# Two hybrid mixer and MLP layers: a smaller scratch for dynamic transfers, deeper buffers, and a new order at the turn, in the tails and in the last chunk

## The chip, the cores and the metric

The kernel runs on one core of a Trainium2 chip. The metric is the device time of one launch in microseconds. A core has five engines, each with a queue of its own that it works through in order: PE (TensorE, matrix products), DVE (VectorE), ACT (ScalarE), POOL (GpSimd) and SP (SyncE, which here issues every transfer).

## The reference

768 tokens of width 1024 (256 of a context, 512 latent) go through two layers. In the last layer only the latent tokens are put out.

```python
for i in range(DEPTH):
    mix_l, mix_c = mixer(modulate(x_l, sh1_l, sc1_l), modulate(x_c, sh1_c, sc1_c), ...)
    x_l = layer_norm(ALPHA * x_l + g1_l * mix_l)
    x_l = layer_norm(ALPHA * x_l + g2_l * sq_relu_mlp(modulate(x_l, sh2_l, sc2_l), w1[i], w2[i]))
    # the context tokens likewise, but not in the last layer
```

The mixer projects its input once and splits it. One part is a conformer convolution: a gate, a depthwise convolution of 31 taps, a layer norm and swish. The other is a state-space scan (SSD) in both directions, over chunks of 128 tokens, in four groups of four heads: per chunk an intra-chunk product with a decay matrix, and a product of the chunk's C with the state of the chunks before it, in either direction. The scan's output is gated, normed per group, joined with the convolution's and projected back. The MLP squares a ReLU between two products of 1024 x 4096.

## The kernel before, in words

All products keep float32 accuracy: each operand is split into a high and a low part, and a product is three matmul passes. A weight goes through four steps as a *unit* of 128x1024: SP loads it into a tile `raw` (two of them), ACT casts the high part into `spl` or `splx` (L346), DVE or POOL subtracts it for the low part (L347), PE uses both.

The program is written as one sequence, and a scheduler with priorities lays it out per engine; a tile pool's `bufs` says how many copies of a tile may be alive, so it sets how early a producer may run. Small steps are put into a list (`later`) and taken off it at each `tick` between blocks of matmuls. The order on each engine is fixed when the program is built.

The stages, by their time in the profile: the modulation and first products (to 48 us), mixer of layer 0 (48 to 422), its *tail* (422 to 486), in which the last group's scan runs beside the first products of the output projection (`pa<-spl,cr`, L935), output projection (to 583), MLP of layer 0 (to 1107), the *turn* (1107 to 1177: the norm of the last MLP chunk, the split input `Hc` and `Hl` of layer 1, and the first products of its mixer), mixer of layer 1 (to 1441), its tail (to 1486), output projection (to 1562), MLP (to 1890) and the end.

The tiles that matter here. `xb` is a chunk's x and B with tokens on partitions, `fb` the feature-wise B or C of a group. `b` (tag b0) and `E` are the two directions' decay matrices of a chunk; SP loads their rows (L747), ACT takes the exponentials (L750, L754). `xd` holds x times the decay for the states (L728, on POOL), and under the same tag `to` holds a chunk's product with the states times its decay (L783, on DVE). `y` is a chunk's output:

```python
y  = x * cbd                  # POOL, L787
y += to[:, d] for each d        # L790: POOL, in the last group (g == 3) DVE
y += pd                         # DVE, L791; pd is the intra-chunk product in PSUM
y *= gz                         # DVE, L792; then its squares on ACT (L795)
```

Then POOL takes a group norm's `rsy`, ACT scales y (L804), PE transposes it (L811), ACT stores it (L711).

In the MLP, hidden units go through in eight chunks. In the last layer's chunk 7 the gate row `gr` is multiplied into the four w2 units (L340, on POOL, called the fold), so that the output needs no multiplication by the gate; the folded tile is `raw`. The row norm after an output projection or an MLP takes statistics on DVE (`bst`, `bve`), the reciprocal root `rsy` on POOL (L366), scales the rows on ACT (L876) and transposes them on PE (L886) into `Hc` or `Hl` by `to_feature`.

Of the kernel before, what the change touches and what calls it, by code (L numbers as in the profile page):

```python
# [7 lines left out]
F32 = mybir.dt.float32  # L8
# [14 lines left out]
DEPTH = 2  # L23
# [4 lines left out]
NPV = 288  # L28
HALVED = 228

GZB, XBB, YB, EB, TB, FXB, FBB, XDB, B0B, RAWB = 4, 6, 4, 3, 2, 2, 3, 2, 2, 2
BGR = 4
SQV = (1, 2, 3)
TAILV = 1
BGP = 100
GSUB = 1
DSUB = "SS"
# [6 lines left out]
FILLM = 4  # L44
MODP = 50
MODLAG = 6
SIDE = 5
FILL = (2, 4)
LOOK = (2, 2)
# [31 lines left out]
def block(ctx, tc, a):  # L81
# [28 lines left out]
    def pb():  # L110
        bank["b"] += 1
        if bank.get("mix"):
            if bank["b"] % 4 == 0:
                return bank["A"].tile([128, 512], F32, tag="A", name="pb")
            return (bank["B"] if bank["b"] % 4 == 2 else psB).tile([128, 512], F32, tag="B", name="pb")
        return (bank["B"] if "B" in bank and bank["b"] % 3 == 0 else psB).tile([128, 512], F32, tag="B", name="pb")
# [121 lines left out]
    def later(lag, fn, group=None):  # L238
        side.append((clock["t"] + lag, fn, group))
# [84 lines left out]

    ostate = {"late": True, "n": 0}

    def emit_unit():
        i = state["next"]
        u = plan[i]
        if u[0] == "out" and state["hid"] is not None and i % 2:  # L330
            raw = state["hid"].tile([128, 1024], F32, tag="raw", name="raw", bufs=2)
        else:
            raw = rawp.tile([128, 1024], F32, tag="raw", name="raw")
        dst = raw
        if u[0] in ("w2", "out"):
            dst = raw.rearrange("p (k c) -> p k c", k=2)
        Q.dma_start(dst, unit_src(u))
        if u[0] == "w2" and u[1] == DEPTH - 1 and u[2] == 7 and FOLD:
            g = state["gate"][:, None, u[3] * 512:(u[3] + 1) * 512].to_broadcast([128, 2, 512])
            (G if FOLD == 1 else V).tensor_tensor(dst, dst, g, op=MUL)  # L340
        state["n"] += 1
        if state["x"] is not None and state["n"] % 4 == 0:
            s = state["x"].tile([128, 2, 1024], F32R, tag="splx", name="splx")
        else:
            s = splp.tile([128, 2, 1024], F32R, tag="spl", name="spl")
# [53 lines left out]
    def mixer(l, full, Hc, Hl, m1, m2, head=None):  # L399
# [313 lines left out]
        def ssd(g, P):  # L713
# [54 lines left out]
            def output(c):  # L768
                Hs = X["H"]
                x = P["XB"][c][:, 0:256]  # L770
                W = X["W"][c]
                pd = pb()
                for h in range(4):
                    T.matmul(pd[:, h * 64:(h + 1) * 64], lhsT=W[:, h], rhs=x[:, h * 64:(h + 1) * 64],
                             start=True, stop=True)
                dirs = [(d, k) for d, k in ((0, c), (1, rev(c))) if k > 0]
                po = pb()
                for d, k in dirs:
                    T.matmul(po[:, d * 256:(d + 1) * 256], lhsT=P["C"][:, c * 128:(c + 1) * 128],
                             rhs=Hs[:, k - 1, d * 256:(d + 1) * 256], start=True, stop=True)  # L780
                d0, d1 = dirs[0][0], dirs[-1][0] + 1
                to = m2.tile([128, 2, 256], F32, tag="xd", name="to", bufs=XDB)
                V.tensor_tensor(to[:, d0:d1].rearrange("p d (h e) -> p d h e", h=4),  # L783
                                po[:, d0 * 256:d1 * 256].rearrange("p (d h e) -> p d h e", h=4, e=64),
                                D["ecs"][:, d0:d1, c, hs:hs + 4, None].to_broadcast([128, d1 - d0, 4, 64]), op=MUL)
                y = m2.tile([128, 256], F32, tag="y", name="y", bufs=YB)
                G.tensor_tensor(y.rearrange(h4, h=4), x.rearrange(h4, h=4),  # L787
                                X["cbd"][c][:, 0:4, None].to_broadcast([128, 4, 64]), op=MUL)
                for d, _ in dirs:
                    E2.tensor_tensor(y, y, to[:, d], op=ADD)  # L790
                V.tensor_tensor(y, y, pd[:, 0:256], op=ADD)  # L791
                V.tensor_tensor(y, y, P["gz"][c // 2][:, (c % 2) * 256:(c % 2 + 1) * 256], op=MUL)  # L792
                if c % 2 == 0:
                    X["ss"][c // 2] = m2.tile([128, 2], F32, tag="ssq", name="ssq", bufs=3)
                S.activation(to[:, 0], y, AF.Square, scale=1.0 / 16, accum_out=X["ss"][c // 2][:, c % 2:c % 2 + 1])  # L795
                X["y"][c] = y
# [78 lines left out]
        for j in range(2):  # L875
            S.activation(rts[j], rts[j], AF.Identity, bias=nb[:, j:j + 1], scale=y[:, j:j + 1])  # L876

    def to_feature(rts, Hd, t0, AB, group):
        n = 256

        def piece(k2):
            tp = pb()
            for i in range(2):
                kt = 2 * k2 + i
                for j, rt in enumerate(rts):
                    T.transpose(tp[:, i * 256 + j * 128:i * 256 + (j + 1) * 128], rt[:, kt * 128:(kt + 1) * 128], ident)  # L886
            for i in range(2):
                tmp = small.tile([128, 512], F32, tag="misc", name="tmp")
                split_h(Hd, 2 * k2 + i, t0, n, tp[:, i * 256:i * 256 + n], AB[0], AB[1], tmp[:, :n],
                        nB=AB[2])  # L890

        for k2 in range(4):
            later(0, lambda k2=k2: piece(k2), group)


    def outproj(l, cats, is_ctx, t0, pairs, xsrc, xdst, op, o2, group):
# [90 lines left out]
    def mlp(l, Hc, Hl, begin, residual, finish, fp):  # L987
# [33 lines left out]
        for ch in range(8):  # L1021
            hid = []
            if ch == RBEG:
                begin()
            if ch == 0:
                ws = []
                for m in range(4):
                    w = weight(("w1", l, m), 0)
                    ws.append(w)
                    hd = new_hid()  # L1030
                    hid.append(hd)
                    ps = pa()
                    parts = []
                    if Hc is not None:
                        cols(ps[:, 0:256], w, Hc, 0, 256)
                        parts.append((ps[:, 0:256], 0, 256))
                        tick(False)
                    cols(ps[:, 256:512], w, Hl, 0, 256)
                    parts.append((ps[:, 256:512], n0, n0 + 256))
                    act(hd, parts, 0, n0 + 256, m)  # L1040
                    tick(False)
                flush("h")
                for m in range(4):
                    ps = pa()
                    cols(ps[:, 0:256], ws[m], Hl, 256, 512)
                    act(hid[m], [(ps[:, 0:256], n0 + 256, n)], n0 + 256, n, m)
                    tick(False)
            else:
                for m in range(4):
                    w = weight(("w1", l, ch * 4 + m))  # L1050
                    hd = new_hid()
                    hid.append(hd)
                    parts = []
                    if Hc is not None:
                        ps = pa()
                        cols(ps[:, 0:256], w, Hc, 0, 256)
# [127 lines left out]
    for l in range(DEPTH):  # L1184
# [19 lines left out]
        with tc.tile_pool(name=f"x_{l}", bufs=1, reuse_waits="tile") as sx, \  # L1204
# [77 lines left out]
            def finish(t, ac, ps, hf, sl):  # L1282
# [26 lines left out]
                    nH["c"] = hp.tile([128, 8, 2, NCX], F32R, tag="Hc", name="Hc")  # L1309
                elif "l" not in nH:  # L1310
                    nH["l"] = hp.tile([128, 8, 2, NL], F32R, tag="Hl", name="Hl")
                for j in range(2 if p > 0 or l + 1 < DEPTH - 1 else 0):
                    rt = o2.tile([128, DM], F32, tag="r", name="xn", bufs=RB)
                    G.tensor_tensor(rt, mine[j], late["lg"], op=MUL)
                    G.tensor_tensor(rt, rt, late["lb"], op=ADD)
                    Q.dma_start(x2[(2 * p + j) * 128:(2 * p + j + 1) * 128, :], rt)
                to_feature(mine, nH["c" if p == 0 else "l"], max(0, p - 1) * 256, late["AB"][min(p, 1)], "h")

            state["hid"] = None
            op.release()  # L1320
# [2 lines left out]
            mlp(l, None if last else Hc, Hl, rows2, residual, finish, fp)  # L1323
            state["x"] = None
            if not last:
                Hc, Hl = nH["c"], nH["l"]
                xcur = x2
        fp.release()
# [53 lines left out]
def build(arrays):  # L1382
    import concourse.bacc as bacc

    nc = bacc.Bacc("TRN2", target_bir_lowering=False, num_devices=1)
    a = {k: nc.dram_tensor(k, v.shape, mybir.dt.from_np(v.dtype), kind="ExternalInput").ap() for k, v in arrays.items()}
    a["out"] = nc.dram_tensor("out", (NL, DM), F32, kind="ExternalOutput").ap()
    with tile.TileContext(nc) as tc:
        block(tc, a)
    return nc  # L1390
# [9 lines left out]
```

## Time and profile before

| | us |
|---|---|
| median of 3 runs | 1938.45 (1932.27 to 1938.45) |
| the profiled execution | 1936.09 |
| its span, first to last instruction | 1934.3 |
| PE busy | 1833.6 (95%) |
| DVE, ACT, POOL busy | 1240.1, 834.5, 523.7 |

A busy share is a mean over stages. A wait is the idle time of an engine ahead of an instruction, with the instruction that ended it. [...]

### The profile page before, as it was taken

The numbers are of one execution on the slowest core, as the hardware profiler recorded it, in microseconds if no ns is written. First come the engines' busy times: TensorE is split into PE (matmuls) and PEld (weight loads), VectorE is DVE, ScalarE is ACT, GpSimd is POOL, SyncE is SP. The second block draws the span as 40 slices with busy tenths as digits, with TensorE's granted clock in tenths as the row PEclk, the third lists the DMA queues.
The fourth block names the chain that finished last, engine by engine and source line by source line (L and its number), as shares of the span: only waits on it lengthen the run. The fifth ranks groups of instructions, "written<-read, shape, count | busy, mean of one in ns | idle before, by whom it ended". The sixth has DMA issues, their size and how long they took to land. (4 is left out here: it accounts for less than half of the span.)

```text
span 1934.3 us, 25688 instructions
## 1 busy us (share of the span) xinstructions
PE 1833.6 (95%) x9832; PEld 1509.5 (78%) x9832; DVE 1240.1 (64%) x1899; ACT 834.5 (43%) x1722; POOL 523.7 (27%) x450
## 2 busy tenths in 40 slices
PE   7999999988999999999999989999998999999997
PEld 4778878775778788888888867888876788888885
DVE  4898969758466145545536567988867764444465
ACT  3636556576375222112212245674674653222322
POOL 2234444433342000000003262555551030000035
PEclk9999999999999999999999999999997999999999
DMA  7434333444653334433412322232232643323331
GB/s 306 138 111 147 103 124 119 140 121 132 239 187 118 117 108 131 142 99 109 142 55 85 105 77 69 89 91 93 77 100 99 237 138 102 104 87 98 98 125 66
DMA packets 119371, 233.53 MB, mean 121 GB/s; under 512 B 7768, under 2 KB 52440, under 8 KB 115152
## 3 DMA queue, kind: packets, MB, share of 16 engines
q1 hardware_dynamic: 119248, 231.90, 36.5%
q8 instruction: 77, 1.26, 0.3%
q14 instruction: 46, 0.38, 0.1%
HBM read 221.15 MB, written 10.72 MB: 120 GB/s over the span
## 5 line engine op out<-in xcount | busy, mean ns | idle before, releaser
L346 ACT CAST spl<-raw 128x1024 fp32r<-128x1024 f32 x196 | 204.7, 1044 | 365.4 <-PE pa L1016 225.6
L1016 PE MATMUL pa<-spl,hid 128*128 128x512 f32 x1440 | 355.7, 398 | 4.9 <-DVE hid L1001 2.8
L1016 PEld LDWEIGHTS pa<-spl,hid 128*128 128x128 f32 x1440 | 269.3, 189 | 78.7 <-ACT hid L999 5.3
L347 DVE TENSOR_TENSOR spl<-raw,spl 128x1024 fp32r<-128x1024 f32 x126 | 162.6, 1292 | 195.7 <-ACT spl L346 195.5
L1009 PE MATMUL pa<-Hl,spl 128*128 128x512 f32 (+1 forms) x1296 | 271.1, 367 | 0.9 <-DVE spl L347 0.7
L383 PE MATMUL pa<-Hl,spl 128*128 128x512 f32 x1104 | 270.3, 396 | 1.2 <-DVE tmp L1287 1.2
L1009 PEld LDWEIGHTS pa<-Hl,spl 128*128 128x128 f32 x1296 | 223.2, 189 | 40.7 <-DVE spl L347 0.9
L383 PEld LDWEIGHTS pa<-Hl,spl 128*128 128x128 f32 x1104 | 203.5, 189 | 51.0 <-issue 9.2
L347 POOL TENSOR_TENSOR spl<-raw,spl 128x1024 fp32r<-128x1024 f32 x70 | 169.3, 2419 | 256.3 <-ACT spl L346 248.0
L548 DVE SCALAR_TENSOR_TENSOR pc<-vp,pv,pc 128x768 f32<-128x768 f32 (+1 forms) x232 | 205.2, 884 | 3.4
L1000 POOL TENSOR_TENSOR rl<-rl 128x512 f32<-128x512 f32 (+2 forms) x18 | 27.1, 1506 | 583.0 <-ACT hid L999 574.3
L1072 DVE TENSOR_TENSOR acc<-acc,pa 128x512 f32<-128x512 f32 x120 | 81.9, 686 | 119.8 <-PE pa L1016 119.7
L997 ACT ACTIVATE rl<-pa 128x256 f32<-128x256 f32 (+1 forms) x104 | 51.3, 498 | 228.0 <-PE pa L1009 224.5
L935 PE MATMUL pa<-spl,cr 128*128 128x512 f32 x540 | 140.7, 409 | 3.6 <-DVE cr L915 1.2
L935 PEld LDWEIGHTS pa<-spl,cr 128*128 128x128 f32 x540 | 101.7, 193 | 33.0 <-DVE cr L915 3.6
L1016 PE MATMUL pa<-splx,hid 128*128 128x512 f32 x480 | 126.5, 398 | 0.0
L383 PE MATMUL pa<-Hc,spl 128*128 128x256 f32 x816 | 118.0, 295 | 0.7 <-ACT t L525 0.7
L383 PEld LDWEIGHTS pa<-Hc,spl 128*128 128x128 f32 x816 | 106.0, 194 | 4.6 <-issue 1.7
L1016 PEld LDWEIGHTS pa<-splx,hid 128*128 128x128 f32 x480 | 90.7, 190 | 21.8
L347 DVE TENSOR_TENSOR splx<-raw,splx 128x1024 fp32r<-128x1024 f32 x42 | 53.3, 1269 | 76.0 <-ACT splx L346 75.9
L691 PE MATMUL pa<-spl,Hl 128*128 128x256 f32 x768 | 97.7, 285 | 0.0
L691 PEld LDWEIGHTS pa<-spl,Hl 128*128 128x128 f32 x768 | 93.7, 191 | 0.1
(229 smaller groups left out, 2866.3 us busy)
## 6 DMA issues: line engine op xcount, KB each, us to landing
mraw<-w_mod SPq DMA_DIRECT2D x40, 1024.0 KB, 5.4
raw<-w1c SPq DMA_DIRECT2D x64, 512.0 KB, 3.4
raw<-w SPq DMA_DIRECT2D x64, 512.0 KB, 3.6
raw<-w_col SPq DMA_DIRECT2D x48, 512.0 KB, 3.5
raw<-w_out SPq DMA_DIRECT2D x48, 512.0 KB, 5.6
b<-cs SPq DMA_DIRECT2D x40, 256.0 KB, 3.5
E<-cs SPq DMA_DIRECT2D x40, 256.0 KB, 4.0
w<-w_m SPq DMA_DIRECT2D x8, 1024.0 KB
```

The source lines that it names most:

```text
L346: S.copy(s[:, 0], raw)
L347: sub_engine(u, i).tensor_tensor(s[:, 1], raw, s[:, 0].bitcast(F32), op=SUB)
L383: T.matmul(ps[:, :n], lhsT=w[:, x, kt * 128:(kt + 1) * 128], rhs=H[:, kt, y, :], start=(kt == 0 and i == 0), stop=(kt == 7 and i == 2))
L548: V.scalar_tensor_tensor(o if j == KCONV - 1 else run["o"], vp[:, :, j:j + GRID], cw[:, j:j + 1], run["o"], op0=MUL, op1=ADD)
L691: T.matmul(ps[:, cc_ * 256:(cc_ + 1) * 256], lhsT=H[:, kt, y, o:o + 128], rhs=w[:, x, k4 * 256:(k4 + 1) * 256], start=(kt == 0 and i == 0) ...
L935: T.matmul(ps[j], lhsT=cr[:, y, j * 128:(j + 1) * 128], rhs=w[:, x, k * 512:(k + 1) * 512], start=(kp == OPAIRS[l][0] and k == 0 and i == ...
L997: S.activation(rl[:, a0 - c0:a1 - c0], p, AF.Relu)
L1000: (V if m_ in SQV else G).tensor_tensor(rl[:, :m], rl[:, :m], rl[:, :m], op=MUL)
L1009: T.matmul(ps, lhsT=w[:, x, kt * 128:(kt + 1) * 128], rhs=H[:, kt, y, t0:t1], start=(kt == 0 and i == 0), stop=(kt == 7 and i == 2))
L1016: T.matmul(ps, lhsT=hid[k][:, y, t * 128:(t + 1) * 128], rhs=ws[k // 2][:, x, (k % 2) * 512:(k % 2 + 1) * 512], start=(k == 0 and i == 0), ...
L1072: V.tensor_tensor(acc[:, t, sl], acc[:, t, sl], ps, op=ADD)
```

## The change

The program is built with `dynamic_dma_scratch_size=1024` in place of the default, which is larger. The freed space goes to buffers: xb 6 to 7, y 4 to 6, E 3 to 4, fb 3 to 4, xd 2 to 3, b0 2 to 3 (layer 1 has its own numbers for xb, fb and gz, which stay).

In the last group of both layers (`PEADD`), `y += to[:, d]` is left out on DVE, and PE adds `to` into the PSUM bank `pd` by a product with the identity. At the turn, the pieces of `to_feature` are put into the list ahead of the steps that multiply out the normed rows (`xn`, now in the list too), and what is left in the list is run at the end of layer 0. In layer 1 the four w2 units of chunk 7 are loaded into one tile `wl` in the place of `Hc` (whose last reader is the last group's xbc product), and folded there; `emit_unit` takes them from it.

```diff
-GZB, XBB, YB, EB, TB, FXB, FBB, XDB, B0B, RAWB = 4, 6, 4, 3, 2, 2, 3, 2, 2, 2
+GZB, XBB, YB, EB, TB, FXB, FBB, XDB, B0B, RAWB = 4, 7, 6, 4, 2, 2, 4, 3, 3, 2
+PEADD = (1, 1)
...
+    def fetch_last():
+
+        t = hp.tile([128, 4, 1024], F32, tag="Hc", name="wl")
+        for k, (hf, i) in enumerate((hf, i) for hf in range(2) for i in range(2)):
+            u = ("w2", DEPTH - 1, 7, hf, i)
+            held_raw[plan.index(u)] = t[:, k]
+            fetch(u, t[:, k])
...
+        if i in held_raw:
+            raw = held_raw.pop(i)
...
+                byT = g == 3 and PEADD[l]
                 for h in range(4):
                     T.matmul(pd[:, h * 64:(h + 1) * 64], lhsT=W[:, h], rhs=x[:, h * 64:(h + 1) * 64],
-                             start=True, stop=True)
+                             start=not byT or h == 0, stop=not byT)
...
                 for d, _ in dirs:
-                    E2.tensor_tensor(y, y, to[:, d], op=ADD)
+                    if byT:
+                        T.matmul(pd[:, 0:256], lhsT=ident, rhs=to[:, d], start=False, stop=d == dirs[-1][0])
+                    else:
+                        E2.tensor_tensor(y, y, to[:, d], op=ADD)
...
             if ch == RBEG:
                 begin()
+                if l == DEPTH - 1:
+                    fetch_last()
...
-                for j in range(2 if p > 0 or l + 1 < DEPTH - 1 else 0):
+                to_feature(mine, nH["c" if p == 0 else "l"], max(0, p - 1) * 256, late["AB"][min(p, 1)], "h", PLAG[p])
+
+                def keep(j):
                     rt = o2.tile([128, DM], F32, tag="r", name="xn", bufs=RB)
...
+                for j in range(2 if p > 0 or l + 1 < DEPTH - 1 else 0):
+                    later(0, lambda j=j: keep(j), "h")
...
             if not last:
+                flush("h")
...
-    nc = bacc.Bacc("TRN2", target_bir_lowering=False, num_devices=1)
+    nc = bacc.Bacc("TRN2", target_bir_lowering=False, num_devices=1, dynamic_dma_scratch_size=1024)
```

The scheduler decides where these steps stand. On POOL, at the start of layer 1's MLP, before (`rl` is a hidden unit's square, `rsy` the rstd of the second half of the output projection's rows, `xt` the residual rows):

```order
L1000 TENSOR_TENSOR rl<-rl 128x256
L366 TENSOR_TENSOR rsy<-bve,nhalf 128x2
L1254 TENSOR_TENSOR xt<-xt,lg 128x512
L1255 TENSOR_TENSOR xt<-xt,lb 128x512
L1254 TENSOR_TENSOR xt<-xt,lg 128x512
```

and with the change:

```order
L1022 TENSOR_TENSOR rl<-rl 128x256
L338 TENSOR_TENSOR wl<-wl,gr_15322 128x1024
L384 TENSOR_TENSOR rsy<-bve,nhalf 128x2
L338 TENSOR_TENSOR wl<-wl,gr_15322 128x1024 x3
L1278 TENSOR_TENSOR xt<-xt,lg 128x512
L1279 TENSOR_TENSOR xt<-xt,lb 128x512
```

One fold stands ahead of `rsy` and three behind it. The four folds of `raw` that stood on POOL in chunk 7, around its last `rl`, are gone.

On PE, in the tail of layer 1, before (`pb<-xb,E` is the intra-chunk product into `pd`, `pb<-hst,fb` the product with the states, `pb<-cst,y` a transpose of y, `pa<-cst,sq` the conformer norm's sums):

```order
L774 MATMUL pb<-xb,E 128x64 x4
L779 MATMUL pb<-hst,fb 128x256 x2
L758 MATMUL pb<-fb 128x128
L779 MATMUL pb<-hst,fb 128x256 x2
L774 MATMUL pb<-xb,E 128x64 x4
L758 MATMUL pb<-fb 128x128
L779 MATMUL pb<-hst,fb 128x256 x2
L774 MATMUL pb<-xb,E 128x64 x8
L811 MATMUL pb<-cst,y 128x128 x4
L779 MATMUL pb<-hst,fb 128x256 x2
L581 MATMUL pa<-cst,sq 128x2 x8
```

and with the change:

```order
L776 MATMUL pb<-fb 128x128
L810 MATMUL pb<-to,cst 128x256 x2
L798 MATMUL pb<-hst,fb 128x256
L793 MATMUL pb<-xb,E 128x64 x4
L798 MATMUL pb<-hst,fb 128x256
L793 MATMUL pb<-xb,E 128x64 x4
L599 MATMUL pa<-cst,sq 128x2 x4
L810 MATMUL pb<-to,cst 128x256 x2
L833 MATMUL pb<-cst,y 128x128 x4
L798 MATMUL pb<-hst,fb 128x256 x2
L599 MATMUL pa<-cst,sq 128x2 x4
L810 MATMUL pb<-to,cst 128x256 x2
```

Each pair of `pb<-to,cst` stands behind the product with the states that `to` is made from, and ahead of the next products; the sums are taken in two parts.

On PE, at the end of the tail of layer 0, before (`pa<-spl,cr` are products of the output projection, `pm<-mraw` those of the modulation):

```order
L779 MATMUL pb<-hst,fb 128x256 x2
L935 MATMUL pa<-spl,cr 128x512 x6
L774 MATMUL pb<-xb,E 128x64 x4
L935 MATMUL pa<-spl,cr 128x512
L811 MATMUL pb<-cst,y 128x128 x4
L169 MATMUL pm<-mraw,cst_90 32x512 x4
L811 MATMUL pb<-cst,y 128x128 x4
L169 MATMUL pm<-mraw,cst_90 32x512
L935 MATMUL pa<-splx,cr 128x512 x24
```

and with the change:

```order
L957 MATMUL pa<-spl,cr 128x512 x4
L810 MATMUL pb<-to,cst 128x256 x2
L798 MATMUL pb<-hst,fb 128x256 x2
L833 MATMUL pb<-cst,y 128x128 x4
L957 MATMUL pa<-spl,cr 128x512 x2
L810 MATMUL pb<-to,cst 128x256 x2
L957 MATMUL pa<-spl,cr 128x512 x11
L833 MATMUL pb<-cst,y 128x128 x2
L957 MATMUL pa<-spl,cr 128x512
L833 MATMUL pb<-cst,y 128x128 x2
L957 MATMUL pa<-spl,cr 128x512 x6
```

The last four transposes, which stood with none of the output projection's products ahead of them but one, stand behind eleven of them.

On SP, the loads of `wl` stand behind the first `b` of the last group of layer 1 and ahead of its first `E` and the second unit of w_out; the load of the gate row stands where it did.

## Rows read from the trace of the kernel before

**Rows 1.** Busy time, share of the span and number of instructions of each engine.

```profile
PE 1833.6 (95%) x9832; PEld 1509.5 (78%) x9832; DVE 1240.1 (64%) x1899; ACT 834.5 (43%) x1722; POOL 523.7 (27%) x450
```

**Rows 2.** Busy time by stage: window, its length, then for PE, PEld, DVE, ACT and POOL the busy time and the number of instructions, the granted clock, DMA's share and GB/s.

```profile
48.00:422.00 374.00, 352.99 (x2262) 296.90 (x2262) 308.05 (x495) 213.57 (x551) 152.02 (x144) 1.00 0.39 125
422.00:486.00 64.00, 51.78 (x248) 36.71 (x246) 47.59 (x95) 37.90 (x100) 21.31 (x24) 0.88 0.46 141
...
1177.00:1441.00 264.00, 252.80 (x1569) 222.61 (x1567) 223.34 (x385) 160.55 (x399) 127.69 (x117) 0.99 0.28 86
1441.00:1486.00 45.00, 37.10 (x165) 27.21 (x166) 33.69 (x70) 27.18 (x74) 15.52 (x20) 0.85 0.19 65
...
1890.00:1934.00 44.00, 29.96 (x121) 23.28 (x119) 26.36 (x43) 7.87 (x10) 21.04 (x17) 0.90 0.20 72
```

**Rows 3.** Waits: engine, what it was about to write and its line, what it waited for, the sum, how many, the longest. First ACT in the mixer of layer 0, then in that of layer 1; then PE in layer 0 and in layer 1.

```profile
ACT b L750 <- DMA b<-cs: 15.0, 5, 4.9
...
ACT b L750 <- DMA b<-cs: 22.8, 7, 7.9
...
PE pb L811 <- ACT y L804: 2.4, 3, 1.3
...
PE pb L811 <- ACT y L804: 2.2, 2, 2.0
```

**Rows 4.** The tails. Groups by line (count, busy, mean ns, idle before): DVE's adds of `to` in tail 0 and tail 1, PE's products with the states in tail 0 and tail 1. Then the timeline (start, length, engine, line, operation, idle before it and what ended it) of PE in tail 0, a window behind its last stall (columns as in rows 2), and the timeline of ACT and DVE in tail 1.

```profile
L790 DVE TENSOR_TENSOR y<-y,to 128x256 f32<-128x256 f32 x10 | 4.6, 464 | 0.4
...
L790 DVE TENSOR_TENSOR y<-y,to 128x256 f32<-128x256 f32 x8 | 3.3, 418 | 0.0
...
L779 PE MATMUL pb<-hst,fb 128*128 128x256 f32 x20 | 6.6, 450 | 0.0
...
L779 PE MATMUL pb<-hst,fb 128*128 128x256 f32 x16 | 5.6, 470 | 2.2 <-DVE y L791 0.8 <-DVE hst L741 0.8 <-DVE to L783 0.6
...
472.22 1.03 PE L779 MATMUL pb<-hst,fb 128*128 128x256 f32 x4
...
483.30 1.15 PE L811 MATMUL pb<-cst,y 128*128 128x128 f32 x4 [4.02 <-ACT y L804]
...
483.30:486.30 3.00, 2.99 (x6) 0.75 (x6) 0.01 (x1) 2.12 (x4) 0.00 (x0) 0.50 0.86 236
...
1453.53 0.70 ACT L750 ACTIVATE b<-b,d_u 128x128 f32<-128x128 f32 x2 [3.09 <-DMA b<-cs]
...
1448.63 0.69 DVE L738 TENSOR_TENSOR hst<-hst,d_x 128x512 f32<-128x512 f32 x1 [2.43 <-ACT hst L735]
...
1468.70 0.69 DVE L577 TENSOR_TENSOR sq<-sq 128x512 f32<-128x512 f32 x1 [0.64 <-ACT sq L575]
```

**Rows 5.** The turn: timeline of POOL, DVE and PE, with the turn's last stall and the window behind it (columns as in rows 2).

```profile
1143.39 0.71 POOL L366 TENSOR_TENSOR rsy<-bve,nhalf 128x2 f32<-128x2 f32 x1
...
1142.08 1.22 DVE L868 TENSOR_SCALAR bve<-bmv 128x2 f32<-128x2 f32 x1
...
1145.62 0.90 PE L886 MATMUL pb<-cst,acc 128*128 128x128 f32 x3 [4.32 <-ACT acc L876]
...
1167.29 0.90 PE L886 MATMUL pb<-cst,acc 128*128 128x128 f32 x3 [2.55 <-ACT acc L876]
...
1167.30:1171.00 3.70, 3.70 (x15) 3.20 (x16) 2.05 (x3) 2.91 (x4) 1.14 (x1) 0.54 0.30 122
```

**Rows 6.** Chunk 7 of layer 1: timeline of POOL, ACT, DVE and PE; the last row is PE in chunk 6.

```profile
1893.82 2.39 POOL L340 TENSOR_TENSOR raw<-raw,gr 128x1024 f32<-128x1024 f32 x1 [3.12 <-DMA raw<-w]
...
1896.24 1.05 ACT L346 CAST spl<-raw 128x1024 fp32r<-128x1024 f32 x1 [4.12 <-POOL raw L340]
...
1878.80 1.22 DVE L347 TENSOR_TENSOR spl<-raw,spl 128x1024 fp32r<-128x1024 f32 x1
...
1897.32 2.50 DVE L347 TENSOR_TENSOR spl<-raw,spl 128x1024 fp32r<-128x1024 f32 x1 [3.43 <-ACT spl L346]
...
1897.87 0.51 PE L1016 MATMUL pa<-spl,hid 128*128 128x512 f32 x1 [0.97 <-ACT hid L999]
1901.20 3.88 PE L1016 MATMUL pa<-spl,hid 128*128 128x512 f32 x9 [2.83 <-DVE hid L1001]
...
1906.79 4.36 PE L1016 MATMUL pa<-spl,hid 128*128 128x512 f32 x18
...
1851.06 12.85 PE L1016 MATMUL pa<-spl,hid 128*128 128x512 f32 x54
```

**Rows 7.** The start of layer 1's MLP: timeline of POOL, PE and SP; then from the page's list of DMA issues (count, KB each, median us from issue to landing) the loads of w1 and of the norms' rows.

```profile
1564.94 0.81 POOL L366 TENSOR_TENSOR rsy<-bve,nhalf 128x2 f32<-128x2 f32 x1 [2.35 <-DVE bve L868]
1575.34 1.29 POOL L1254 TENSOR_TENSOR xt<-xt,lg 128x512 f32<-128x512 f32 x1 [9.60 <-DMA xt<-x]
...
1567.27 0.55 PE L886 MATMUL pb<-cst,r 128*128 128x128 f32 x3 [0.39 <-ACT r L876]
...
1560.81 0.33 SPq L857 DMA_DIRECT2D gr<-grow  x1
...
raw<-w1c SPq DMA_DIRECT2D x64, 512.0 KB, 3.4
...
lg<-lnr SPq DMA_DIRECT2D x4, 512.0 KB, 6.3
lb<-lnr SPq DMA_DIRECT2D x4, 512.0 KB, 4.3
```

More of the change, by code (lines that the diff above doesn't have):

```diff
@@ L46 @@
 MODLAG = 6
+PLAG = (0, 0, 0)
 SIDE = 5
@@ L325, in block, with fetch @@
     ostate = {"late": True, "n": 0}
[L327 to L333, printed above, removed]
+    held_raw = {}
+    def fetch(u, raw):
         dst = raw
@@ L340, in emit_unit @@
             (G if FOLD == 1 else V).tensor_tensor(dst, dst, g, op=MUL)
+    def fetch_last():
[4 more added lines that the diff above has]
+            fetch(u, t[:, k])
+    def emit_unit():
+        i = state["next"]
+        u = plan[i]
+        if i in held_raw:
+            raw = held_raw.pop(i)
+        elif u[0] == "out" and state["hid"] is not None and i % 2:
+            raw = state["hid"].tile([128, 1024], F32, tag="raw", name="raw", bufs=2)
+            fetch(u, raw)
+        else:
+            raw = rawp.tile([128, 1024], F32, tag="raw", name="raw")
+            fetch(u, raw)
         state["n"] += 1
@@ L789, in output @@
                 for d, _ in dirs:
-                    E2.tensor_tensor(y, y, to[:, d], op=ADD)
+                    if byT:
+                        T.matmul(pd[:, 0:256], lhsT=ident, rhs=to[:, d], start=False, stop=d == dirs[-1][0])
+                    else:
+                        E2.tensor_tensor(y, y, to[:, d], op=ADD)
                 V.tensor_tensor(y, y, pd[:, 0:256], op=ADD)
@@ L876, in row_norm, with to_feature @@
             S.activation(rts[j], rts[j], AF.Identity, bias=nb[:, j:j + 1], scale=y[:, j:j + 1])
-    def to_feature(rts, Hd, t0, AB, group):
+    def to_feature(rts, Hd, t0, AB, group, lag=0):
         n = 256
@@ L892, in to_feature @@
         for k2 in range(4):
-            later(0, lambda k2=k2: piece(k2), group)
+            later(lag, lambda k2=k2: piece(k2), group)
     def outproj(l, cats, is_ctx, t0, pairs, xsrc, xdst, op, o2, group):
@@ L1316, in finish @@
                     Q.dma_start(x2[(2 * p + j) * 128:(2 * p + j + 1) * 128, :], rt)
-                to_feature(mine, nH["c" if p == 0 else "l"], max(0, p - 1) * 256, late["AB"][min(p, 1)], "h")
+                for j in range(2 if p > 0 or l + 1 < DEPTH - 1 else 0):
+                    later(0, lambda j=j: keep(j), "h")
             state["hid"] = None
```

## Prediction

> **What bounds the kernel now.** I read the page's shares first: PE is busy 95% of the span, and no other engine comes near [rows 1]. So time can come only from PE's waits, from stretches at a lower granted clock, or from work taken off PE. The table by stage tells where these are [rows 2]: mixer 0 leaves PE idle 21.0 of 374 us, its tail 12.2 of 64, mixer 1 11.2 of 264, its tail 7.9 of 45, the end 14 of 44 (of which some 10 are the last norm and the last store, with no matmul left); the turn has two waits of 4.32 and 2.55 [rows 5]. The granted clock is 0.88, 0.85 and 0.90 in the tails and at the end, and 0.99 to 1.00 in the mixers. In these short stages PE is not the bound: chains through DVE, ACT and POOL are. All the parts of the change lie there or in the mixers, so at most some 60 us are in play, and each part moves a few.
>
> **The scratch and the buffers.** Every transfer is issued by SP, and the queue that carries them is of the hardware kind; I cost the smaller scratch itself at nothing, because no row shows a user of it. What it buys is one buffer more in xb, E, fb, xd and b0 and two in y (in layer 1, xb, fb and gz keep theirs). In the order the decay loads b and E move one chunk ahead. That serves ACT's waits for b: 15.0 us in mixer 0 and 22.8 in mixer 1 [rows 3]. But ACT is busy 57 to 61% of those stages, so most of that is slack. What ends a late decay on PE is the wait of y's transposes for y: 2.4 us in mixer 0, 2.2 in mixer 1 [rows 3]. Decay is one of several things on the chain to y, so I take half of the 4.6: **-2.3**. Bounds: half of PE's idle time in mixer 1, -5.6, applied to both together, and 0, since DVE at 82 to 85% may be what is late next; I exclude no small loss from reordering, but give it no size.
>
> **The adds on PE.** Ten DVE adds leave tail 0 (4.6 us) and eight tail 1 (3.3 us) [rows 4]. PE gets 18 matmuls of 128x256 on f32. The trace has none by the identity; nearest is the output matmul on hst, four records for two matmuls, 1.03 us at full clock, so 0.5 us each: 5 us in tail 0, 4 in tail 1.
> Tail 0: its longest stall is 4.02 us at 483.30, for y; the matmuls behind it ran at clock 0.50 for 3 us, a loss of 1.5 [rows 4]. In the new order eleven cr matmuls (0.24 us each at full clock, by the eighteen of this shape in [rows 6]) stand ahead of those transposes, and the last four outputs need 8 DVE adds fewer. That is -5.5; of the 5 us of new matmuls I let half fall into the 8 us of other waits: +2.5. **-3.0**. Bounds: -8 (all the new matmuls are hidden and the other waits shrink by 2.5) and +5 (the stall only moves, all new matmuls are on the path).
> Tail 1: DVE works without a wait from 1448.63 to 1468.06 [rows 4], so taking 3.3 us from it shortens the chain by that, less the new hop: `to` goes to PE, and DVE's next add waits for PE. PE's wait for `to` was 0.6 in this tail [rows 4]; I take off twice that, 1.2, and round: **-2.0**. ACT's 3.09 us for b at 1453.53 go too if b comes early, giving -5; +4 if the new matmuls all lie on the path.
>
> **The turn.** PE waits 4.32 us at 1145.62 for the normed rows, and the rstd there starts at 1143.39, right after the statistics on DVE, which ended at 1143.3, their last step taking 1.22 us [rows 5]. Three matmuls of 0.24 us now stand ahead of these transposes and fill some of it: **-0.7**. The statistics end no earlier, so I expect no more; 2 either way as bounds (the last stall of the stage is 2.55 us [rows 5], and it may grow or go).
>
> **The fold, taken from the end.** In chunk 7 the four folds of 2.39 us wait for their loads, ACT's casts wait for the folds (4.12 us), DVE's subtraction for the cast, hid stands behind that on DVE, and PE waits 0.97 and 2.83 us [rows 6]. The nine matmuls after it took 3.88 us; eighteen later ones took 4.36, so nine cost 2.18 and the lower clock 1.7. In chunk 6, with the same loads and no fold, PE runs 54 matmuls on with no wait [rows 6]. **-5.5**. Bounds: -3.8 if the lower clock stays, -5.8 with the 0.3 us that the one matmul between the two waits lost.
>
> The row here also shows DVE's subtraction at 2.50 us beside a fold and 1.22 alone [rows 6]. [...]
>
> **The fold, at its new place.** The order puts the first fold on POOL ahead of the rstd of the second half of layer 1's output projection. POOL is in order, and the fold reads a gate row whose load SP issues at 1560.81 (after the last reader of the row before it), at an unchanged place. Behind the rstd stand ACT's norm and PE's transposes, which waited 0.39 us [rows 7]. Its landing isn't shown; loads of the same 512 KB took 3.4 (raw), 4.3 (lb) and 6.3 us (lg) [rows 7]. I take 4.3, as lb is a row spread over partitions as the gate is. So it lands at 1565.1, the fold ends at 1567.5, and rstd starts then, where it started at 1564.94: 2.6 us later, all of it PE's. The stall becomes 3.0 us. After one of 2.55 us at 1167.29 the clock was 0.54 for 3.7 us [rows 5], a loss of 1.7. **+4.3**. Bounds: a landing after 3.4 us and no clock loss, +1.7; after 6.3 with it, +6.3. The other three folds (7.2 us) fit in the 9.60 us in which POOL waited for xt [rows 7].
> The early loads, 2 MB, stand on SP ahead of E of the first chunk of the last group. DMA was busy 0.28 in mixer 1 and 0.19 in its tail [rows 2], so I cost them at nothing; at 3.4 us each [rows 7], not hidden, they would cost tail 1 up to 14 us.
>
> **Sum.** -2.3 - 3.0 - 2.0 - 0.7 - 5.5 + 4.3 = -9.2, from the profiled 1936.09: 1926.9. The runs' median is 1938.45, from 1932.27, so the profiled one is in their middle. 0.5% (9.7 us) is about what a measurement of this kernel can tell from no change; against the median that line is at 1928.8.
>
> **Rivals.**
> *Nothing in sum.* Mixers and tails are DVE's, what buffers free is slack, the new matmuls eat what the adds gave, and the gate lands after 6.3 us: 1936.09 - 5.5 + 6.3 - 0.7 = 1936.2. For it: only 4.6 us of PE's waits name what the buffers feed. Against it: two of tail 0's and tail 1's adds are on the chain to y.
> *Slower.* The identity matmuls stand in PE's order right where `to` is not ready, and everything behind them waits. Price: 18 matmuls by the tails' own grouped durations (6.6 us for ten, 5.6 for eight, lower clock included [rows 4]) = 12.2, plus a wait for `to` of 0.6 us for each of ten pairs = 6.0. Without the two tails' gains: 1936.09 - 2.3 - 0.7 - 5.5 + 4.3 + 18.2 = 1950.1. It decides once more than 12 us of that is uncovered. For it: PE's order in tail 1 has nothing but such steps. Against it: PE idles 20 us in the two tails.
> *Much faster.* The waits in the tails go with their low clock, buffers give their bound, and the gate lands early: 1936.09 - 8 - 5 - 5.6 - 2 - 5.5 + 1.7 = 1911.7.
>
> **Numbers.** Forecast 0.42, nothing in sum 0.28, slower 0.12, much faster 0.18. The time is that of the likeliest, 1926.9; its own range is 1919 to 1934. With the neighbours, 1912 to 1942 leaves out half of "slower" and a part of "much faster". Faster by over 0.5%: "much faster" and three quarters of the forecast, 0.50. Slower by over 0.5% (above 1948): 0.10. Within: 0.40.
>
> **What would show it.** At the end no PE wait over 1 us in chunk 7 and the nine matmuls at about 0.24 us each; at 1560 to 1570 a PE wait for ACT's r of about 3 us, with rsy behind a fold that waits for the gate's load; in tail 0 no wait of 4 us ahead of the last transposes; ACT's waits for b smaller in both mixers, PE's idle time there 2 to 3 us less. I am wrong if the wait at the transposes is over 6 us, if PE's idle time in the tails grows, or if PE waits in tail 1 for raw w_out or E behind the early loads.

## The result and the profile after

The changed kernel takes 1922.46 us in the median of 10 runs (1917.19 to 1928.95), the kernel before 1932.91 in 10 (1932.2 to 1939.04): a ratio of 0.9938, 95% interval 0.9926 to 0.995. A second comparison, on another occasion, gave 0.9959 (0.9943 to 0.9974). The forecast was 1926.9, in a range of 1912 to 1942. The profiled execution went from 1936.09 to 1923.74 us, 12.35 less, where the sum had 9.2.

The profile after: the span and the clock, the busy times, and the stages of [rows 2] in the same windows (the last one ends with the span). The granted clock is TensorE's, as a share of its full speed; at any one time it is 1.00 or 0.50 in the traces of both kernels, and a figure between them is the mean of a window.

```profile
core 0: 1921.8 us, clock 0.990
...
PE 1827.9 (95%) x9868; PEld 1509.2 (79%) x9868; DVE 1239.1 (64%) x1881; ACT 834.7 (43%) x1722; POOL 520.8 (27%) x450
...
48.00:422.00 374.00, 353.06 (x2276) 298.21 (x2274) 311.12 (x502) 220.24 (x570) 151.38 (x144) 1.00 0.40 129
422.00:486.00 64.00, 59.43 (x291) 44.00 (x291) 39.32 (x82) 33.40 (x86) 21.56 (x26) 0.92 0.44 151
1177.00:1441.00 264.00, 252.51 (x1548) 222.09 (x1544) 222.37 (x378) 167.55 (x424) 130.75 (x123) 0.99 0.31 96
1441.00:1486.00 45.00, 37.32 (x173) 28.39 (x173) 34.50 (x67) 19.90 (x45) 10.41 (x15) 0.92 0.29 100
1890.00:1921.00 31.00, 21.23 (x91) 16.59 (x89) 19.56 (x36) 4.15 (x5) 15.62 (x14) 0.92 0.18 68
```

PE's busy time fell by 5.7 us, although the change gives it 18 matmuls more (36 records); less of its time is at the lower clock, as the granted clock of the tails shows (0.92 in both, before 0.88 and 0.85). In the window of tail 0 PE does 7.7 us more than in [rows 2], and ACT 4.5 us less; ACT does 6.7 more in mixer 0. In tail 1 ACT has 7.3 less, in mixer 1 7.0 more: a part of the decay's exponentials has moved out of the tails. The windows stand still while the kernel got shorter, so a count from a fixed step says more, from the casts of weights that bound the stages below: behind the one at 379.3 us ACT has 112 of its steps on `b` and `E` (L750 a ReLU, L754 the exponential) left in layer 0 before and 96 after, behind the one at 1424.8 us 61 and 45 in layer 1. The 16 that moved are the steps of one chunk. One of the four kinds of these steps in tail 0, before and after, then in tail 1, before and after; the last two rows are ACT's waits for b after, in mixer 0 and mixer 1:

```profile
L750 ACT ACTIVATE b<-b,d_u 128x128 f32<-128x128 f32 x16 | 5.6, 389 | 4.0 <-DMA b<-cs 4.0
...
L768 ACT ACTIVATE b<-b,d_u 128x128 f32<-128x128 f32 x12 | 4.2, 390 | 4.3 <-DMA b<-cs 4.3
...
L750 ACT ACTIVATE b<-b,d_u 128x128 f32<-128x128 f32 x8 | 2.8, 391 | 4.0 <-DMA b<-cs 3.1 <-DVE E L756 0.9
...
L768 ACT ACTIVATE b<-b,d_u 128x128 f32<-128x128 f32 x4 | 1.4, 390 | 3.1 <-DVE hst L759 3.1
...
ACT b L768 <- DMA b<-cs: 19.3, 7, 5.7
...
ACT b L768 <- DMA b<-cs: 20.4, 8, 5.0
```

PE's waits tell the same, with one exception. At the end none is left in chunk 7 (before, 0.97 and 2.83 us [rows 6]), and the longest in tail 0 is 1.37 us, where it was 4.02 [rows 4]. At the start of layer 1's MLP the wait at the transposes has grown from 0.39 us [rows 7] to 4.71. PE's longest wait in tail 0, then the timeline of the end and of that place:

```profile
PE pa L616 <- POOL rsy L384: 1.4, 1, 1.4
...
1883.14 5.60 PE L1031 MATMUL pa<-Hl,splx 128*128 128x512 f32 x24
1888.58 3.98 PE L1038 MATMUL pa<-spl,hid 128*128 128x512 f32 x16
...
1549.02 0.33 SPq L879 DMA_DIRECT2D gr<-grow  x1
...
1552.77 2.93 POOL L338 TENSOR_TENSOR wl<-wl,gr 128x1024 f32<-128x1024 f32 x1 [0.98 <-DMA gr<-grow]
1555.80 0.81 POOL L384 TENSOR_TENSOR rsy<-bve,nhalf 128x2 f32<-128x2 f32 x1
1556.59 8.23 POOL L338 TENSOR_TENSOR wl<-wl,gr 128x1024 f32<-128x1024 f32 x3
...
1553.37 2.35 DVE L890 TENSOR_SCALAR bve<-bmv 128x2 f32<-128x2 f32 x1
...
1556.65 2.29 DVE L896 SCALAR_TENSOR_TENSOR bnb<-bmv,rsy 128x2 f32<-128x2 f32 x1 [0.60 <-POOL rsy L384]
1558.87 1.21 DVE L365 TENSOR_TENSOR splx<-raw,splx 128x1024 fp32r<-128x1024 f32 x1
...
1558.98 2.37 ACT L898 ACTIVATE r<-r,bnb,rsy 128x1024 f32<-128x1024 f32 x2 [6.28 <-DVE bnb L896]
...
1560.27 0.55 PE L908 MATMUL pb<-cst,r 128*128 128x128 f32 x3 [4.71 <-ACT r L898]
...
1560.27:1563.90 3.63, 3.63 (x19) 3.63 (x20) 2.32 (x1) 2.18 (x4) 3.63 (x2) 0.57 0.65 191
```

Read the part from 1549.02 on by its ends. The gate row, issued at 1549.02, is there at 1552.77. The first fold ends at 1555.70. `bve`, a DVE instruction on 128x2 elements that took 0.16 us at this place in the kernel before (at 1564.69) and in e_late (below), with no fold beside it, starts at 1553.37 and ends at 1555.72, with the fold. That costs little by itself, since `rsy` stands behind the same fold on POOL. `rsy` runs; the second fold starts at 1556.59, and `bnb`, as small, lies beside it for 2.29 us. Only then can ACT norm the rows, at 1558.98. Behind the wait the clock was 0.57 for 3.6 us (the last row, with columns as in rows 2).

### The profile page after: what moved, and what is told of

Same layout as the page of the kernel before. It is cut to its first block, busy times and chain, and to the rows that moved or that the text cites. A ratio compares the mean times of both kernels' runs of the same rounds, so it can differ in the third digit from the quotient of the medians.

```text
span 1921.8 us, 25717 instructions
## 1 busy us (share of the span) xinstructions
PE 1827.9 (95%) x9868; PEld 1509.2 (79%) x9868; DVE 1239.1 (64%) x1881; ACT 834.7 (43%) x1722; POOL 520.8 (27%) x450
## 5 line engine op out<-in xcount | busy, mean ns | idle before, releaser
L365 DVE TENSOR_TENSOR spl<-raw,spl 128x1024 fp32r<-128x1024 f32 x123 | 157.4, 1280 | 190.5 <-ACT spl L364 190.1
```

## The experiments

To see where each kernel's time lies, I took the start of every cast of a weight on ACT from the timelines (240 in each kernel, in the same order), and from them the length of each stage. The table gives each kernel's difference to the kernel before in us; its first column is the length before. Stages run from the cast at 100.8 us in the kernel before to those at 379.3, 524.3, 1210.2, 1424.8, 1550.0, 1614.1, 1861.2 us and to the end, so *tail 0* holds the end of mixer 0 and the first half of the output projection.

| stage | before | after | after_again | e_late | e_one | e_noadd | e_best | e_best2 | e_oldbuf | e_bufonly | e_b_decay | e_b_rest | e_turn | e_scratch |
|---|---|---|---|---|---|---|---|---|---|---|---|---|---|---|
| head | 100.8 | 0.4 | 2.5 | 2.0 | 2.2 | 2.7 | 0.4 | 3.4 | 0.3 | 0.6 | -0.1 | 2.8 | 2.4 | 2.5 |
| mixer 0 | 278.5 | -3.2 | -1.2 | -3.3 | -4.2 | -4.1 | -1.6 | -1.7 | -1.7 | -2.0 | -1.5 | -1.4 | -3.7 | -0.1 |
| tail 0 | 145.0 | -4.3 | -4.3 | -2.7 | -4.3 | -6.3 | -6.3 | -4.7 | -2.7 | -4.8 | -3.8 | 1.8 | -2.8 | 1.2 |
| to the turn's end | 685.9 | 0.6 | -2.8 | -2.8 | 1.8 | 0.1 | -1.6 | 2.2 | -5.3 | 0.3 | 1.9 | -2.3 | -0.5 | -1.1 |
| mixer 1 | 214.6 | -0.8 | -2.6 | -1.4 | -0.2 | -0.9 | -2.1 | -1.7 | 0.6 | -1.5 | -0.9 | -1.2 | -0.3 | -0.6 |
| tail 1, output projection | 125.2 | -4.4 | -6.8 | -6.0 | -5.3 | -7.3 | -4.3 | -5.9 | -3.6 | -4.6 | -1.3 | -0.4 | -5.1 | -1.0 |
| MLP 1, start | 64.0 | 5.1 | 6.7 | 1.4 | 2.4 | 4.7 | 0.4 | 0.1 | 5.4 | 0.0 | 0.6 | 3.4 | 5.4 | 0.2 |
| MLP 1 | 247.1 | -0.0 | -0.0 | -0.0 | 0.0 | -0.0 | -0.0 | -0.0 | 0.0 | -0.0 | -0.0 | 0.0 | -0.0 | 0.0 |
| end | 73.1 | -5.7 | -5.7 | -5.7 | -5.7 | -5.7 | -5.8 | -5.7 | -5.8 | 1.2 | -5.8 | -5.8 | -5.7 | 0.6 |
| span | 1934.3 | -12.5 | -14.2 | -18.6 | -13.4 | -16.8 | -20.9 | -14.1 | -12.6 | -10.7 | -10.8 | -3.0 | -10.4 | 1.8 |

Two profiles of the one changed kernel (the first two columns) differ by 2.0 us in mixer 0, 1.8 to 2.4 in mixer 1 and tail 1, 3.4 on the way to the turn's end and 2 in the first 100 us, which nothing changed. One other kernel, profiled twice (e_best and e_best2), differs by 1.6 us in tail 0 and by 3.8 to the turn's end. A good part of what differs to the turn's end is a single wait of PE for `acc`, 2.64 us at 1162.25 in the changed kernel, which one profile of each pair has and the other doesn't. Smaller differences in these stages say nothing alone. The end repeats to 0.1 us. A profile isn't the median either: e_oldbuf's and e_best's are the fastest of their runs (1923.59 where the median is 1928.99, 1915.24 where it is 1918.29), and e_b_rest's is 2.6 us above its median.

**The fold.** Two kernels move it. Both rewrite the gate row on ACT with a zero made from chunk 2's sum, so that nothing that reads it can start before chunk 3:

```diff
+    def folds(acc):
+        z = small.tile([128, 2], F32, tag="bnb", name="zero")
+        V.tensor_scalar(z, acc[:, 0, 0:2], 0.0, None, op0=MUL)
+        S.activation(state["gate"], state["gate"], AF.Identity, bias=z[:, 0:1])
+        while late_folds:
+            fold(*late_folds.pop(0))
...
-            if ch == RBEG:
+            if ch == (3 if l == DEPTH - 1 else RBEG):
                 begin()
                 if l == DEPTH - 1:
                     fetch_last()
+                    folds(acc)
```

In e_late all four folds wait for it, in e_one the first stays where it was. The edited line moves `begin` and `fetch_last` too, but the loads of `wl` are still issued from 1399.7 us in the changed kernel and from 1398.9 in e_late.

e_late: 

> The changed kernel with its four folds moved behind the norm: ACT rewrites the gate row (plus a zero made from chunk 2's sum), and POOL folds only after that, in chunk 3. Theory: the new PE wait of 4.71 us ahead of the transposes is the fold ahead of rsy and the folds beside DVE's small steps. Then that wait falls to about 0.4 us, bve and bnb on DVE take 0.16 us each, and the time is about 5 us below the changed kernel's 1922.5, at 1917 to 1918. Rival: the wait comes from the order of the matmuls or from late statistics after the earlier start of this stage; then the wait stays over 3 us and the time within 1 us of 1922.5.

e_one: 

> Like e_late, but the first fold stays at its place ahead of rsy and only the other three go to chunk 3. Theory: bnb on DVE (2.29 us in the changed kernel, 0.16 before) stood still because a fold ran on POOL; so it falls to about 0.16, the PE wait from 4.71 to about 2.5 us, and about 2 us of the 5 come back (1920 to 1921), while bve, beside the first fold, stays at over 2 us. Rival: only POOL's order counts (rsy behind one fold); then the wait stays at 4.5 to 4.9 us and the time at 1922.5, since the three folds stand behind rsy anyway.

Measured: e_late 0.9921 of the kernel before (0.9907 to 0.9935), e_one 0.9928 (0.9912 to 0.9944). In us, e_late's median is 1919.04, 3.4 below the changed kernel's 1922.46, where I had expected 5; the two were not run beside each other. e_late and e_one aren't told apart by their times, but they are by the rows. First e_late, DVE, POOL and PE; then e_one, with the clock behind its wait.

```profile
1550.44 0.16 DVE L902 TENSOR_SCALAR bve<-bmv 128x2 f32<-128x2 f32 x1
...
1551.52 0.16 DVE L908 SCALAR_TENSOR_TENSOR bnb<-bmv,rsy 128x2 f32<-128x2 f32 x1 [0.60 <-POOL rsy L396]
...
1553.02 0.55 PE L920 MATMUL pb<-cst,r 128*128 128x128 f32 x3 [0.39 <-ACT r L910]
...
1669.00 11.42 POOL L343 TENSOR_TENSOR wl<-wl,gr 128x1024 f32<-128x1024 f32 x4 [20.35 <-ACT gr L348]
```

```profile
1554.28 3.01 POOL L346 TENSOR_TENSOR wl<-wl,gr 128x1024 f32<-128x1024 f32 x1 [0.90 <-DMA gr<-grow]
1557.40 0.81 POOL L399 TENSOR_TENSOR rsy<-bve,nhalf 128x2 f32<-128x2 f32 x1
...
1554.96 2.36 DVE L905 TENSOR_SCALAR bve<-bmv 128x2 f32<-128x2 f32 x1
...
1558.25 0.16 DVE L911 SCALAR_TENSOR_TENSOR bnb<-bmv,rsy 128x2 f32<-128x2 f32 x1 [0.60 <-POOL rsy L399]
...
1559.74 0.55 PE L923 MATMUL pb<-cst,r 128*128 128x128 f32 x3 [2.59 <-ACT r L913]
...
1559.74:1563.00 3.26, 3.26 (x28) 3.18 (x29) 0.23 (x2) 2.62 (x5) 0.00 (x0) 1.00 0.69 167
```

The wait is 0.39 us without folds, 2.59 with the first, 4.71 with all. In e_one `bve` still ends with the fold (1557.32 and 1557.29), while `bnb` is back at 0.16 us. The rival, that only POOL's order counts, would have left 4.71, since the three folds stand behind `rsy` in both. So 2.2 us of the wait are the first fold (the wait for the gate and the fold, with which `bve` ends) and 2.1 the second fold, through `bnb`. The clock behind the wait is 1.00 in e_one, so of the two waits only the longer one of the changed kernel had a loss at the lower clock behind it. The stage behaves alike: +4.7 to +6.7 with all folds there (five profiles), +2.4 with one, +0.1 to +1.4 with none, but for e_b_rest's +3.4 (it and e_late have a wait of 2.5 and 2.2 us for a weight a little later).

**The adds.** e_noadd sets `PEADD = (0, 0)`.

> The changed kernel with the adds of the last group back on DVE (PEADD off in both layers). Theory of the prediction: the adds on PE gave most of what the tails gained (3.2 us in tail 0 and 4.1 in tail 1 by the traces' marks), so 5 to 7 us are lost, 1928 to 1929. Rival: the deeper buffers did that and the adds moved nothing; then the time is within 1.5 us of 1922.5. Second rival: the matmuls cost more than they give; then it is faster, by 2 to 4 us.

Measured: 0.9933 (0.9919 to 0.9948), beside e_late. The theory is out: nothing was lost. Tail 0 is 6.3, 6.3, 4.7 and 4.8 us shorter than before in the four kernels with all the buffers and DVE adds, and 2.7 to 4.3 (five kernels) with the adds on PE, so there the matmuls rather cost about 2 us, hardly more than two profiles of one kernel differ by. The ten matmuls take 5.9 us of PE (the first row below, of the changed kernel). In the whole window 422 to 486 PE is busy 59.43 us in the changed kernel and 55.39 in e_bufonly below, which has the adds on DVE (the second row); that difference, 4.0, holds other matmuls that moved as well. In tail 1 the two kinds overlap.

```profile
L810 PE MATMUL pb<-to,cst 128*128 128x256 f32 x20 | 5.9, 409 | 0.0
...
422.00:486.00 64.00, 55.39 (x258) 40.44 (x258) 44.33 (x93) 33.26 (x85) 20.77 (x25) 0.89 0.47 157
```

**The buffers.** e_oldbuf is the changed kernel with the buffers of before; e_bufonly the kernel before with the new buffers and the scratch, and nothing else.

```diff
-GZB, XBB, YB, EB, TB, FXB, FBB, XDB, B0B, RAWB = 4, 7, 6, 4, 2, 2, 4, 3, 3, 2
+GZB, XBB, YB, EB, TB, FXB, FBB, XDB, B0B, RAWB = 4, 6, 4, 3, 2, 2, 3, 2, 2, 2
```

e_oldbuf: 

> The changed kernel with the six buffer counts of before, the small scratch kept. Theory: the buffers gave the 4.0 us of mixer 0 and 0.8 to 2.3 us of mixer 1 and nothing in the tails; so 5 to 6 us are lost, 1927 to 1929, all before 422 us and in mixer 1. Rival: they also made the tails faster; then 9 to 12 us are lost, 1932 to 1934, and tail 0 has its wait of 4 us again. Second rival: they are slack, within 1.5 us.

e_bufonly: 

> The kernel before with only the smaller scratch and the deeper buffers. Theory: the buffers made both mixers and both tails faster (about 4, 4, 1.5 and 5 us by the marks of the kernel with the adds on DVE), and the end and the start of the second MLP are as before; 10 to 13 us below the kernel before, a ratio of 0.993 to 0.995. Rival: the adds on PE were needed in the tails; then only the mixers' 4 to 6 us, 0.997.

Measured: e_oldbuf 0.9973 (0.9961 to 0.9985), e_bufonly 0.9976 (0.9961 to 0.9992). So the buffers alone, and all the rest alone, gave a quarter of a per cent each. e_bufonly's profile is 10.7 us shorter, where its ratio makes 4.6; a profile is one execution, and its runs lie between 1922.84 and 1934.29. Its gains lie in both mixers and in both tails; I had given the buffers nothing in the tails. e_oldbuf's tails are shorter too, by 2.7 and 3.6 us, so the adds on PE help where the buffers are short, and together the two give no more than the buffers alone. e_oldbuf has no wait of 4 us in tail 0 either: thirteen products of the output projection stand ahead of the last transposes, which wait 0.76 us.

```profile
474.87 3.37 PE L957 MATMUL pa<-spl,cr 128*128 128x512 f32 x13
478.99 0.90 PE L833 MATMUL pb<-cst,y 128*128 128x128 f32 x4 [0.76 <-ACT y L826]
```

So the stall of tail 0 goes by the adds without the buffers, and by the buffers without the adds (in e_bufonly the last transposes wait 0.79 us). e_oldbuf's median of 1928.99 us is the time that I had expected of it, but not with shorter tails; in which stage it loses what the ratios differ by (0.9973 and 0.9938) isn't shown, since its profile is its fastest run.

**Which buffers, and the best of both.** e_best has the folds in chunk 3 and the adds on DVE; e_best2 is the same kernel again. e_b_decay (first line) and e_b_rest (second) are e_best with one half of the buffers.

```diff
+GZB, XBB, YB, EB, TB, FXB, FBB, XDB, B0B, RAWB = 4, 6, 4, 4, 2, 2, 3, 2, 3, 2
+GZB, XBB, YB, EB, TB, FXB, FBB, XDB, B0B, RAWB = 4, 7, 6, 3, 2, 2, 4, 3, 2, 2
```

after_again: 

> The changed kernel as it stands, to be compared on one chip with the three beside it. Every theory: 0.992 to 0.995 of the kernel before.

e_best: 

> Both of what the first experiments showed to cost: the folds in chunk 3 (as in e_late) and the last group's adds on DVE (as in e_noadd). Theory: the fold's place costs 4 to 5 us, and by the stages' marks the adds on PE cost 2 us in tail 0 and 1.5 in tail 1; the two are in different stages and add up, so 6 to 9 us below the changed kernel beside it, a ratio to the kernel before of 0.9900 or less. Rival: the adds on PE are worth nothing either way; then it is as e_late, 4 to 5 us below the changed kernel.

e_best2: 

> e_best once more, as the bound for the two beside it: 0.991 to 0.994 of the kernel before, and below both of them if each half of the buffers does something.

e_b_decay: 

> As e_best (folds in chunk 3, adds on DVE), but of the deeper buffers only those of the decay loads are kept (E 4, b0 3); xb, y, fb and xd are as before. Theory: the tails gained from the decay loads, which come a chunk earlier; so this is as fast as e_best within 2 us, and tail 0 keeps its 6 us against the kernel before. Rival: xd, which also holds `to`, is what the tails waited for; then tail 0 keeps under 3 us and the time is 4 us or more above e_best.

e_b_rest: 

> As e_best, with the other half: xb 7, y 6, fb 4 and xd 3 kept, E 3 and b0 2 as before. Theory of the decay loads: tail 0 keeps under 3 us of its 6, and ACT's wait for b in mixer 1 is over 20 us again; 4 us or more above e_best. Rival (xd): within 2 us of e_best.

Measured: after_again 0.9959; e_best 0.9929 (0.9912 to 0.9945) beside it, and 0.9932 (0.9913 to 0.995) later; e_b_decay 0.9963 (0.9946 to 0.998); e_b_rest 0.9977 (0.9963 to 0.9991). My bound of 0.9900 for e_best was missed. It stands 5.2 us below the changed kernel beside it (1918.29 and 1923.5), which is what the fold alone should give, and e_late with the adds on PE has 0.9921: in the times the adds are worth nothing either way. e_best is quicker than the changed kernel beside it; e_late wasn't run beside it, its ratio is below both of the changed kernel's, and its interval overlaps the first of them (0.9926 to 0.995). I can't tell e_best and e_late apart.

The halves are told apart in tail 0. ACT's work in the window 422 to 486 is 33.30 us with the decay buffers and 37.78 without (mixer 0 the other way, 219.06 and 213.03), and the stall of 4 us of [rows 4] is back in e_b_rest, at 4.88. The count of the first section says the same: behind the cast at 379.3 us 96 steps are left in all ten profiles with the decay buffers, and 112 in e_b_rest, e_oldbuf and e_scratch. Windows of e_b_decay, then windows and timeline of e_b_rest:

```profile
48.00:422.00 374.00, 354.22 (x2272) 297.20 (x2270) 310.36 (x499) 219.06 (x569) 151.54 (x144) 1.00 0.40 128
422.00:486.00 64.00, 54.04 (x255) 38.80 (x255) 46.52 (x93) 33.30 (x85) 21.14 (x25) 0.92 0.44 145
```

```profile
48.00:422.00 374.00, 354.26 (x2271) 299.95 (x2270) 304.55 (x488) 213.03 (x548) 151.68 (x144) 0.99 0.38 122
422.00:486.00 64.00, 53.91 (x252) 39.34 (x251) 50.31 (x101) 37.78 (x101) 21.34 (x26) 0.88 0.48 151
...
485.35 1.15 PE L845 MATMUL pb<-cst,y 128*128 128x128 f32 x4 [4.88 <-ACT y L838]
```

ACT's wait for b in mixer 1, by which I had meant to tell them apart, is 20.2 us in e_b_rest, but 20.4 in the changed kernel too, with all the buffers. So the theory of the decay loads holds for tail 0 (-3.8 against +1.8 us). Its other half falls: alone they give tail 1 only 1.3 us of 4.3 to 5.9, although their 16 steps have left it as well, and e_b_decay is 4.6 us slower than e_best2 beside it, e_b_rest 9.0. By one profile of each, tail 1 needs the decay buffers and at least one of the others; which one wasn't tried (in layer 1 it can only be y or xd, since xb and fb have their own numbers there).

**The turn and the scratch.** e_turn puts the steps of `to_feature` and `xn` back in their old order.

e_turn: 

> The changed kernel with the turn's steps in the order of before. By the marks the turn of the changed kernel moved by under 1 us against the kernel before (predicted 0.7 us faster). Theory: the order moves nothing that bounds the turn, since the statistics on DVE end no earlier; within 1 us of the changed kernel beside it, with PE's wait at the turn at 4.0 to 4.4 instead of 3.2 us and the rest of it given back behind it. Rival: it gave 1.1 us there, and the time is 1 to 2 us longer.

Measured: 0.9954 (0.9937 to 0.9972), and 0.9959 for the changed kernel beside it. The wait at the turn is 3.20 us in the changed kernel and 4.31 in e_turn, so the three matmuls do fill it, but the time shows nothing of 1.1 us. First the changed kernel, then e_turn:

```profile
1140.19 0.55 PE L908 MATMUL pb<-cst,acc 128*128 128x128 f32 x3 [3.20 <-ACT acc L898]
...
PE pb L908 <- ACT acc L898: 6.4, 3, 3.2
```

```profile
1142.63 0.90 PE L908 MATMUL pb<-cst,acc 128*128 128x128 f32 x3 [4.31 <-ACT acc L898]
...
PE pb L908 <- ACT acc L898: 7.5, 3, 4.3
```

e_scratch: 

> The kernel before with the smaller scratch alone; its instructions stand in the same order on every engine. Theory: nothing uses the scratch, 0.998 to 1.002 of the kernel before. Rival: it changes the transfers, and the loads' times to landing and the time move by over 0.3%.

Measured: 0.9999 (0.9987 to 1.0012). The scratch costs and gives nothing by itself.

## Why the prediction was right, and where

The time, the sign and the size hold, but in part by luck: of the six terms only the largest came as it was worked out. One was right in kind and too small, one can't be measured, one isn't shown, and the two of the tails came near by a cause that was half of the truth.

- *The fold taken from the end, -5.5.* Right: the stage is 5.7 to 5.8 us shorter in all eleven profiles that have the early load, and not in e_bufonly and e_scratch. No wait is left, and where nine matmuls took 3.88 us in the kernel before, at a granted clock of 0.57 (the window 1901.20 to 1905.08), sixteen take 3.98 us, at 1.00 (1888.58 to 1892.56).
- *The fold at its new place, +4.3.* Right in kind, too small. I had 2.6 us of waiting and 1.7 of clock; it is 4.3 of waiting more, the clock behind it fell as I had it (0.57 for 3.6 us), and the stage lost 4.7 to 6.7. The gate landed after 3.7 us, earlier than the 4.3 I took. The step that failed is what a fold does to DVE, which is in no term of the sum, though I had a row of it: the subtraction of 2.50 us beside a fold and 1.22 alone [rows 6]. In the changed kernel the folds struck the two smallest instructions of the norm, each held until a fold ended (2.35 and 2.29 us for 0.16). `bve` was held beside a fold that `rsy` had to wait for anyway; `bnb` was not, and its 2.1 us lie on the chain to PE. I had a second row of it: the `bve` of 1.22 us at the turn [rows 5], which I read as a long statistic. It ended at 1143.30, and POOL's two subtractions beside it at 1143.28. In which way the two engines hold each other up, no run shows.
- *The mixers by the buffers, -2.3.* The sign agrees, the cause isn't shown: nine kernels with all the buffers have -1.2 to -4.2 in mixer 0 and -0.2 to -2.6 in mixer 1, but e_oldbuf, without them, has -1.7 in mixer 0, and two profiles of one kernel differ by as much. PE's idle time in the two windows, which I expected 2 to 3 us smaller, stayed (21.0 and 11.2 us before, 20.9 and 11.5 after). And the step behind the term failed. ACT's wait for b did not shrink (15.0 us in [rows 3], 19.3 after; 22.8 and 20.4 in mixer 1). What moved is ACT's work, out of the tail.
- *The tails by the adds, -3.0 and -2.0.* Forecast near the marks (-4.3 and -4.4), and without the buffers the adds do about that (-2.7 and -3.6 in e_oldbuf, with the products of the output projection ahead of the last transposes as I had it). But the buffers without the adds do it too (-4.8 and -4.6 in e_bufonly), and I had put them at nothing there; with them, the adds on PE give nothing in the times and rather cost about 2 us in tail 0. I had seen that DVE worked without a wait in tail 1 and took DVE's adds for the bound. I hadn't asked how much of the tail's work could be done before the tail began.
- *The turn, -0.7.* Within what can't be measured; its wait fell by 1.1 us.

Of the rivals, *nothing in sum* and *slower* fell, and *much faster* too. The price of the matmuls (5.9 us of PE time in tail 0, where I had 5) fell in great part into waits, as I let it. The early loads, which I costed at nothing, are seen in one wait of ACT for E (3.39 us at 1411.88; 2.18 in e_bufonly, which doesn't have them) and in no wait of PE beside it over 1.6 us, where before the longest was 1.3. One thing that no step had is left open: chunk 6 of layer 0's MLP is 1.4 us longer in most of the kernels and not in e_noadd and e_oldbuf, with a wait of 1.67 us at 1063.77 for DVE's acc; I didn't follow it.

The best that came of it is e_late or e_best: about 0.7% below the kernel before, where the change has 0.4 to 0.6%.

## What to carry to other kernels

Ahead of a tail, look for work that depends on nothing in it (here the exponentials of the decay) and count the buffers that hold it back; here that made it needless to take instructions off the engine that looks busy in the tail. And try two changes to one stage each alone before adding up what they give: here either took the same stall. When a large GpSimd instruction is moved to where GpSimd is idle, look at what VectorE does there, the small steps on a chain above all: here a step of 0.16 us lasted 2.29 beside a fold of 2.34. Take the price of a moved instruction at the new place by its neighbours on every engine, not only by its queue.

## What I had not expected of the hardware

VectorE and GpSimd looked as if they took turns in whole instructions: in the changed kernel three folds that take 2.39 us each [rows 6] lasted 8.23 us, 1.06 more, and DVE's subtraction of 1.21 us, in no way slowed (1.22 alone [rows 6]), lies right behind the end of the second fold (1558.93), where `bnb` ends too; behind it a product on DVE of 128x256 took 2.59 us, where one of the same line took 0.42 at 1551.82; four folds in a row in chunk 3 of e_late took 11.42 us.

The clock did not follow the length of a wait alone. Behind the wait of 4.71 us it was 0.57, behind that of 2.55 us 0.54 [rows 5], and behind the 2.59 us of e_one it was 1.00.
